# Two wide layers' second product as three sweeps of seven block products, with weight sums added up in DRAM

## The chip, the cores and the metric

The kernel runs on one core of a Trainium2 chip. The time is device microseconds (us) of that core, as the median of several runs. TensorE (PE) does the matmuls, VectorE (DVE), ScalarE (ACT) and GpSimd (POOL) the elementwise work; SyncE (SP), ACT and POOL can issue DMAs.

## What is computed

Two layers of an encoder over 512 tokens of width 1024, in float32. Cut to what matters:

```python
for layer in range(DEPTH):                       # 2
    hn = rmsnorm(h, norm_mix[layer])
    h = h + (hybrid_attention(hn, ...) if layer % 2 == 0 else neighbourhood_attention(hn, ...))
    h = h + sq_relu_mlp(rmsnorm(h, norm_ffn[layer]), ffn_w_up[layer], ffn_w_down[layer])
return rmsnorm(h, final_norm)

def sq_relu_mlp(h, w_up, w_down):                # (512, 1024) x (1024, 4096) x (4096, 1024)
    u = jax.nn.relu(h @ w_up)
    return (u * u) @ w_down
```

"First product" is `h @ w_up`, "second product" is `(u * u) @ w_down`; these are the wide layers.

## The kernel before

Activations lie transposed in SBUF: `hT` holds 8 blocks of 128 features by 512 tokens. Every float32 factor is split into a rounded high part (ACT) and a remainder (DVE or POOL), and a product is three matmuls: high by high, high by low, low by high (lines 500 to 503). 30 slots of 128 x 1024 numbers (`Slot`) hold what lives longer; weights come through `raw`, `whi` and `wlo`. `weights` (line 237) loads five chunks ahead and splits two ahead of the one in use.

The plain form (`product`, line 415) multiplies a 128 x 128 weight block by all 512 tokens. The seven-product form (`Seven`, line 314) takes two 128-row blocks of the sum, two column blocks and two token halves together, as a 2 x 2 block product with seven multiplications in place of eight, each by 256 tokens. For it POOL makes the sums of weight blocks (lines 302 to 304) and of the tokens (336 to 340), and DVE and ACT put the seven results together (396 to 400).

`mlp` (line 1250) goes in stages, by `SIZES`. Layer 0 makes 6 blocks of 128 rows of `u` plainly and multiplies them plainly with `w_down`; then 8 more blocks by the seven-product form, multiplied plainly; then 8 more plainly multiplied and 10 kept, which `convert` turns into five pairs for four runs of the seven-product form, one for every 256 output columns. In layer 1 it is 6, 8 and 6 blocks plainly, 8 in the seven-product form, and 4 at the very end with the tokens as the stationary factor (`down`, line 1621), together with the final norm.

The order within each engine's queue is set by the framework's scheduler, which may move an instruction ahead of others as long as its data allow it; only layer 1's attention (`fixed_order`, line 957) and single instructions (`keep_in_program_order`) stand as written. All DMAs of one engine are issued in the order of its queue, and an instruction that waits holds up all that stand behind it on its engine. Layer 0's attention (`attend`, line 961) works through 64 steps: scores (TensorE), row minimum (DVE), exponential (ACT), reciprocal (DVE), scaling of `p` by it (POOL, line 1005), transposes and values (TensorE). Between the steps `fill` puts matmuls of projections.

Of the kernel before, what the change touches and what calls it, by code (L numbers as in the profile page):

```python
# [35 lines left out]
def encoder_kernel(ctx: ExitStack, tc: tile.TileContext, ins, out, dbg=None):  # L36
# [738 lines left out]

    kst = Slot()
# [312 lines left out]

    fill.add("z", product(w_in, 0, XP, tiles(768, 384), ev_cq, three))  # L1090
# [4 lines left out]
    attend(all_heads(), step)  # L1095
    fill.until("out")
# [11 lines left out]
    SIZES = (6, 8, 8, 10), (6, 8, 6, 8, 4)  # L1108

    def first_product(l):  # L1110
# [10 lines left out]
        state = dict(c=SIZES[l][0], ids=None, plain=False, split=iter(()))  # L1121
# [68 lines left out]
        def stage(n, raw=0, more=0):  # L1190
# [4 lines left out]
            while left:  # L1195
# [5 lines left out]
                for _ in x7.run(i, raw_evac if more <= left < more + raw else pair_evac):  # L1201
                    pass
# [40 lines left out]
    def convert(u7, R):  # L1243
        held = tc.keep_in_program_order
        for kp, raw in enumerate(R):
            yield from u7.sums(kp, raw, DVE, held)
            yield
            yield from u7.split(kp, held)

    def mlp(l, last=None):  # L1250

# [6 lines left out]
        beside = lambda m, i: None  # L1258
        k0 = 0
        for z, n in enumerate(SIZES[l][:3]):  # L1260
            U, R, V = stage(n, *(SIZES[l][3:] if z == 2 else ()))
            up = [s_.pair() for s_ in U]

            def ev(m, b):
                DVE.tensor_tensor(hT[:, m, :], hT[:, m, :], b, op=ALU.add)

            gens = [product(w, k0, up, tiles(512 * c, 512), lambda j, b, c=c: ev(4 * c + j, b)) for c in range(2)]
            k0 += n
            work = iter(())
            if z == 2:  # L1270
                u7 = Seven(2 * len(R))
                ids = [u7.plan(w, 256 * m, k0) for m in range(4)]
                if last:
                    beside = last(k0 + 2 * len(R), V)
                reserve[0] = 8
                work = convert(u7, R)
            else:
                ahead()
            for c, gen in enumerate(gens):
                for i, _ in enumerate(gen):  # L1280
                    if z == 0:
                        later(c, i)
                    elif z == 1:
                        next(bias, None)
                    next(work, None)
            for _ in work:
                pass
            reserve[0] = 1
            for s_ in U:
                s_.free()  # L1290
        for m in range(4):

            def evac(w_):
                h2 = hT[:, 2 * m : 2 * m + 2, :]
                DVE.tensor_tensor(h2, h2, w_.t.rearrange("p (z n) -> p z n", z=2), op=ALU.add)

            for i, _ in enumerate(u7.run(ids[m], evac)):
                beside(m, i)
        u7.free()

    mlp(0)


# [273 lines left out]
    def last_mlp():  # L1577
# [43 lines left out]
        def down(k0, c, up, tail):  # L1621
# [5 lines left out]
            def run():  # L1627
# [27 lines left out]
        def last(k0, tiles_):  # L1655
# [4 lines left out]
            def beside(m, i):  # L1660
                if m == 2 and i == 0:
# [3 lines left out]
                if m > 1 and i in (16, 22):  # L1665
                    turn(2 * (m - 2) + (i == 22), 0)
# [3 lines left out]
        mlp(1, last)  # L1670
# [58 lines left out]
```

## Time and profile before

| | |
|---|---|
| median of 3 runs | 1183.78 us (1182.7 to 1184.34) |
| span of the profiled execution | 1184.0 us |
| TensorE busy, share of the span | 98% |
| VectorE, ScalarE, GpSimd busy | 75%, 54%, 44% |
| granted TensorE clock, mean | 0.994 |
| bytes moved by DMA | 128.01 MB |
| layer 0's attention with its projections | to about 268 us |
| layer 0's wide layer | about 268 to 604 us |
| layer 1's attention | about 604 to 828 us |
| layer 1's wide layer and final norm | about 828 us to the end |

A page of the profile gives busy time by engine, then the DMA queues (q1 is that of SP, q0 of POOL, q10 of ACT), then the chain that ended last and the costliest groups. A group's row reads: line, engine, operation, output and inputs, shape, count, then busy time in all and mean of one in ns, then idle time before it and what ended that. A timeline's row gives the start and the duration first, and in brackets the idle time before it. A windows row gives for a stretch the busy us and the count for each engine, then the granted clock, the share of the DMA engines that was busy, and GB/s.

### The profile page before, as it was taken

To read this page: it belongs to the slowest core of one execution; us is meant where nothing else is said; L and a number is where in the kernel's file an instruction comes from. 1 tells how busy PE (TensorE), PEld (TensorE's weight loads), DVE (VectorE), ACT (ScalarE), POOL (GpSimd) and SP (SyncE) were. 2 spreads that over 40 slices of the span, in tenths; PEclk is the share of its full clock that TensorE was granted. 3 is DMA by queue.
4 is the path that set the end of the run, shared out by engine and by line. 5 is a ranking of instruction groups with operands and counts; after the bars stand their busy time and mean duration, and the time that the engine had idled before them with its cause. 6 is when DMAs were issued, how large, how long until landed. Compare 5 with 4: busy or idle time off the path is not lost.

```text
span 1184.0 us, 19784 instructions
## 1 busy us (share of the span) xinstructions
PE 1160.5 (98%) x7128; PEld 1021.2 (86%) x7128; DVE 883.2 (75%) x1514; ACT 640.3 (54%) x1081; POOL 526.1 (44%) x662
## 2 busy tenths in 40 slices
PE   9989999999999999999999999999999999999997
PEld 8667778888899899988998998988889989998895
DVE  5788998878967368786884676667996736778975
ACT  4468676664546247562553565555554624666344
POOL 3267343224562377819602232231376625774710
PEclk9999999999999999999999999999999999999998
DMA  7223225212524723225226464433352341322412
GB/s 244 71 54 92 68 78 134 62 56 77 167 86 134 263 70 90 72 90 165 67 72 178 131 184 126 116 112 109 107 165 76 115 134 55 98 64 89 143 36 71
DMA packets 110145, 128.01 MB, mean 108 GB/s; under 512 B 9075, under 2 KB 86816, under 8 KB 110048
## 3 DMA queue, kind: packets, MB, share of 16 engines
q1 hardware_dynamic: 106992, 119.30, 33.5%
q0 software_dynamic: 2304, 6.31, 2.2%
q8 instruction: 56, 0.92, 0.3%
q10 hardware_dynamic: 752, 1.15, 0.3%
q14 instruction: 41, 0.34, 0.1%
HBM read 104.32 MB, written 6.29 MB: 93 GB/s over the span
## 4 chain that ended last, share of the span: by engine, by line
PE 81%; DVE 4%; ACT 1%; issue 1%; POOL 0%; DVEq 0%; ACTq 0%
PE mm L503 8%; PE mm L501 8%; PE mm L502 8%; PE mm L390 4%; PE mm L389 4%; PE mm L388 4%; PE t L388 3%; PE t L389 3%; PE t L390 3%; PE s L502 2%; PE s L503 2%; PE s L501 2%; PE s L390 2%; PE s L388 2%; PE s L389 2%; PE s L997 2%
## 5 line engine op out<-in xcount | busy, mean ns | idle before, releaser
L309 DVE TENSOR_TENSOR wlo<-a,whi 128x896 fp32r<-128x896 f32 x132 | 161.8, 1230 | 83.7 <-ACT whi L308 82.9
L308 ACT ACTIVATE whi<-a 128x896 fp32r<-128x896 f32 x132 | 125.0, 950 | 155.0 <-PE o L502 45.8
L501 PE MATMUL mm<-a,whi 128*128 128x512 f32 x485 | 195.9, 406 | 0.9 <-DVE a L915 0.7
L503 PE MATMUL mm<-a,wlo 128*128 128x512 f32 x485 | 192.1, 397 | 2.5 <-DVE wlo L202 2.5
L502 PE MATMUL mm<-a,whi 128*128 128x512 f32 x485 | 192.5, 397 | 0.1
L202 DVE TENSOR_TENSOR wlo<-raw,whi 128x1024 fp32r<-128x1024 f32 (+4 forms) x117 | 139.3, 1193 | 66.4 <-ACT whi L212 63.9
L212 ACT ACTIVATE whi<-raw 128x1024 fp32r<-128x1024 f32 (+3 forms) x120 | 116.4, 971 | 92.2 <-PE s L502 39.8
L302 POOL TENSOR_TENSOR a<-a 128x128 f32<-128x128 f32 x132 | 85.1, 645 | 173.3 <-DMA a<-in_ffn_w_up_dram 103.9
L303 POOL TENSOR_TENSOR a<-a 128x256 f32<-128x256 f32 x132 | 120.2, 910 | 10.3
L304 POOL TENSOR_TENSOR a<-a 128x128 f32<-128x128 f32 x132 | 115.1, 872 | 10.3
L503 PEld LDWEIGHTS mm<-a,wlo 128*128 128x128 f32 x485 | 91.7, 189 | 23.7 <-DVE wlo L202 3.4
L501 PEld LDWEIGHTS mm<-a,whi 128*128 128x128 f32 x485 | 91.8, 189 | 20.4 <-PE t L972 0.9
L502 PEld LDWEIGHTS mm<-a,whi 128*128 128x128 f32 x485 | 91.9, 190 | 17.4 <-DVE a L545 0.4
L388 PE MATMUL mm<-a,whi 128*128 128x256 f32 x370 | 103.9, 281 | 0.0
L389 PE MATMUL mm<-a,whi 128*128 128x256 f32 x370 | 103.9, 281 | 0.0
L390 PE MATMUL mm<-a,wlo 128*128 128x256 f32 x370 | 103.7, 280 | 0.0
L1005 POOL TENSOR_SCALAR p<-p,ti 128x512 f32<-128x512 f32 x64 | 46.2, 724 | 92.3 <-DVE ti L1004 81.1
L1430 POOL TENSOR_SCALAR p<-p,ti 128x256 f32<-128x256 f32 x64 | 35.6, 567 | 104.8 <-DVE ti L1429 91.8
L388 PE MATMUL t<-a,whi 128*128 128x256 f32 x264 | 74.2, 281 | 0.0
L389 PE MATMUL t<-a,whi 128*128 128x256 f32 x264 | 74.1, 281 | 0.0
L390 PE MATMUL t<-a,wlo 128*128 128x256 f32 x264 | 73.9, 280 | 0.0
L390 PEld LDWEIGHTS mm<-a,wlo 128*128 128x128 f32 x370 | 69.6, 188 | 0.2 <-DVE wlo L309 0.2
(338 smaller groups left out, 3210.8 us busy)
## 6 DMA issues: line engine op xcount, KB each, us to landing
a<-in_ffn_w_up_dram SPq DMA_DIRECT2D x104, 256.0 KB
raw<-in_ffn_w_down_dram SPq DMA_DIRECT2D x46, 512.0 KB
raw<-in_od_w_qkv_dram SPq DMA_DIRECT2D x64, 128.0 KB
a<-in_ffn_w_down_dram SPq DMA_DIRECT2D x28, 256.0 KB
raw<-in_ffn_w_up_dram SPq DMA_DIRECT2D x12, 512.0 KB
raw<-in_ev_w_in_dram SPq DMA_DIRECT2D x12, 384.0 KB
a<-a SPq DMA_DIRECT2D x18, 256.0 KB
bias<-bx SPq DMA_DIRECT2D x16, 256.0 KB
```

The costliest lines, as they stand in the source:

```text
L202: z = lambda: (eng or DVE).tensor_tensor(to, src, f32(high), op=ALU.subtract)
L212: ACT.activation(hi[:, 0:m], raw[:, 0:m], AF.Copy)
L303: POOL.tensor_tensor(r[:, 4:6], r[:, 2:3].to_broadcast([P, 2, P]), r[:, 0:7:6], op=ALU.add)
L304: POOL.tensor_tensor(r[:, 7], r[:, 3], r[:, 5], op=ALU.subtract)
L308: ACT.activation(hi[:, 0:896], raw[:, 128:1024], AF.Copy)
L309: DVE.tensor_tensor(lo[:, 0:896], raw[:, 128:1024], f32(hi[:, 0:896]), op=ALU.subtract)
L388: PE.matmul(o, wh, x[:, 0], start=kp == 0 and n in (0, 1, 3, 5), stop=False, skip_group_check=True)
L389: PE.matmul(o, wh, x[:, 1], start=False, stop=False, skip_group_check=True)
L390: PE.matmul(o, wl, x[:, 0], start=False, stop=kp == self.np - 1, skip_group_check=True)
L501: PE.matmul(o, wh, xh, start=first, stop=False)
L502: PE.matmul(o, wh, xl, start=False, stop=False)
L503: PE.matmul(o, wl, xh, start=False, stop=last)
```

## The change

The second product takes six blocks of `u` plainly, as before, and all others (26 in layer 0, 22 in layer 1; in layer 1 four more go to `down` as before) in the seven-product form, in one go: two 128-row blocks by the two halves of the 1024 output columns by two token halves. A pair of blocks needs 7 products with four column blocks each. They are done in three sweeps over all pairs (`kind` 0, 1, 2 with two, two and three products), and each sweep leaves sums in the banks X, Y and Z that later go to `hT`. So the first product makes all its 26 remaining blocks in one row of 13 runs.

The weight sums of the sweeps are made in DRAM, in a copy `made` of the weights: for each pair ACT copies 256 rows (1 MB) from DRAM to DRAM, and POOL issues four DMAs of 256 rows by 256 columns x 2 (0.26 MB) that add to what stands there, two from the weights and two from blocks of `made` itself. There are 13 + 11 pairs. The code asks for one add at each step of layer 0's attention from the fifth step on (layer 0's pairs), and for layer 1's adds beside layer 0's wide layer. POOL no longer makes sums for the second product. The token sums (`one` to `four`) and remainders are on VectorE. The transposes of layer 1's end (`turn(j, 0)`) move from the old last run into `down`.

```diff
+    FIRST, RAW, MORE = 6, (26, 22), (0, 4)
...
+    class SumsAhead:
+            self.made = dr.tile([n, 2, P, 1024], F32, name=nm("made"))
...
+        def steps(self):
+            todo = []
+            for kp in range(self.n + 4):
+                if kp < self.n:
+                    k = self.k0 + 2 * kp
+                    ACT.dma_start(self.made[kp].rearrange("z p c -> (z p) c"), self.w[k * P : (k + 2) * P, :])
+                for back, z, f, src in ((2, 1, 1, lambda q: self.weight(q, 0, 1)), (2, 0, 1, lambda q: self.weight(q, 0, 0)),
+                                        (3, 0, 0, lambda q: self.block(q, 1, 1)), (4, 1, 0, lambda q: self.block(q, 0, 0))):
+                    if 0 <= kp - back < self.n:
+                        POOL.dma_start(self.block(kp - back, z, f), src(kp - back), accum_op=ALU.add)
+                        yield
...
+        if n > 3:
+            next(sums0, None)
+    ahead0, ahead1 = (SumsAhead(ins["ffn_w_down"][l], FIRST, RAW[l] // 2) for l in range(2))
+    sums0, sums1 = ahead0.steps(), ahead1.steps()
...
-    SIZES = (6, 8, 8, 10), (6, 8, 6, 8, 4)
...
+    def sweep_chunk(w, k0, kind, made):
...
+        if kind == 0:
+            for z in range(2):
+                SP.dma_start(line(a[:, S * z : S * z + S]), half(k0 + z, 0))
+        else:
+            for z in range(2):
+                SP.dma_start(line(a[:, S * z : S * z + S]), blocks(made[z])[:, (z, 1 - z)[kind - 1]])
+        if kind == 2:
+            SP.dma_start(line(b[:, 0:S]), half(k0 + 1, 1))
...
+        ACT.activation(hi, a, AF.Copy)
+        DVE.tensor_tensor(lo, a, f32(hi), op=ALU.subtract)
+        third = None
+        if kind == 2:
+            third = Slot()
+            ACT.activation(third.t[:, 0:S], b[:, 0:S], AF.Copy)
+            DVE.tensor_tensor(third.t[:, S:], b[:, 0:S], f32(third.t[:, 0:S]), op=ALU.subtract)
...
+    class Sweeps:
...
+        def tokens(self, kind, kp):
...
+            if kind == 0:
+                split_to(d[:, :, 0], d[:, :, 1], r[:, 0:4:2])
+                self.one(kp)
+                if kp < 2:
...
+            elif kind == 1:
+                for q, src in enumerate((r[:, 0], s2)):
+                    split_to(d[:, q, 0], d[:, q, 1], src)
+                if kp + 2 < self.n:
+                    self.two(kp + 2)
+                if kp + 2 >= self.n:
+                    self.three(kp + 2 - self.n)
+                    self.four(kp + 2 - self.n)
...
+        def run(self, R):
...
+            PRODUCTS = [
+                [(X, 0, at(0)), (Z, 1, at(S))],
+                [(Y, 0, at(S)), (X, 1, at(0))],
+                [(Y, 2, at(S)), (Z, 1, lambda h, m: (h[2].t[:, 0:S], h[2].t[:, S:], P * m)), (X, 0, at(0))],
+            ]
...
+                PE.matmul(o, wh, x[:, 0], start=first and m % 2 == 0, stop=False, skip_group_check=True)
+                PE.matmul(o, wh, x[:, 1], start=False, stop=False, skip_group_check=True)
+                PE.matmul(o, wl, x[:, 0], start=False, stop=last, skip_group_check=True)
...
+            steps = [(kind, kp) for kind in range(3) for kp in range(self.n)]
...
-        for z, n in enumerate(SIZES[l][:3]):
...
+    def mlp_swept(l, made, last=None, sums=iter(())):
...
+        reserve[0] = 3
+        sweeps = []
+        R = stage(0, RAW[l] + MORE[l], 0, lambda: sweeps.append(Sweeps(w, FIRST, made)), lambda: next(sums, None))[1]
...
+        for n, (kind, kp) in enumerate(sweeps[0].run(R)):
+            beside(kind, kp)
+            if n % 16 == 15:
+                next(rest, None)
+            if n % 4 == 0:
+                next(sums, None)
...
+    mlp_swept(0, ahead0, None, sums1)
...
+                if c == 0:
+                    for j in range(4):
+                        turn(j, 0)
...
+            def beside(kind, kp):
+                if (kind, kp) == (2, 6) and not H:
...
+        mlp_swept(1, ahead1, last)
+        flip[0] = 1
```

How the scheduler laid this out is seen in the built programs. First ACT's queue at the program's start, before (`whi` and `a` are high parts, `raw` loaded weights):

```order
L111 DMA cst<-in_cst_dram 128x182
L112 DMA a_82<-in_norm_mix_dram 16x128
L140 ACT_TABLE_LOAD
L140 ACTIVATE ti_109<-zeros 128x1
L1649 ACT_TABLE_LOAD
L1649 ACTIVATE ti_12779<-ones 128x1
L143 ACTIVATE gT<-t_111 128x16
L544 ACTIVATE a_114<-t_155,gT 128x512
L212 ACTIVATE whi_150<-raw_148 128x768
```

and the same place now (`made_621` is layer 0's copy of the weights, `made_622` layer 1's):

```order
L111 DMA cst<-in_cst_dram 128x182
L112 DMA a_82<-in_norm_mix_dram 16x128
L140 ACT_TABLE_LOAD
L140 ACTIVATE ti_109<-zeros 128x1
L802 DMA made_621<-in_ffn_w_down_dram 16x16384 x2
L143 ACTIVATE gT<-t_111 128x16
L212 ACTIVATE whi_150<-raw_148 128x768
L544 ACTIVATE a_114<-t_155,gT 128x512
L544 ACTIVATE a_115<-t_167,gT 128x512
L802 DMA made_621<-in_ffn_w_down_dram 16x16384
L212 ACTIVATE whi_177<-raw_175 128x768
```

The copies (L802) stand between the first loads' splits; 20 of the 24 are issued before ACT takes up `raw_654`, a chunk of the projection that follows the first six column blocks.

POOL's queue behind its first small loads, with the semaphores that each row waits for, before:

```order
L130 DMA a_82<-in_final_norm_dram 8x128
L517 ISA
L517 TENSOR_TENSOR acc_122<-acc_122,sc_248 128x512 [waits Activation_49]
L517 TENSOR_TENSOR acc_122<-acc_122,sc_283 128x512 [waits Activation_49,Pool_49]
L517 TENSOR_TENSOR acc_122<-acc_122,sc_318 128x512 [waits Activation_49,Pool_49]
```

and now (DMAHW are the semaphores of SP's and ACT's DMAs, DMASW those of POOL's, eight of each in turn; a row with `in_ffn_w_down_dram` adds weights, one with `made` on both sides adds a block of the copy):

```order
L130 DMA a_82<-in_final_norm_dram 8x128
L806 DMA made_621<-in_ffn_w_down_dram 256x256 [waits DMAHW5_49,DMASW0_49]
L806 DMA made_621<-in_ffn_w_down_dram 256x256 [waits DMASW1_49]
L806 DMA made_621<-in_ffn_w_down_dram 256x256 [waits DMAHW0_49,DMASW2_49]
L806 DMA made_621<-in_ffn_w_down_dram 256x256 [waits DMASW3_49]
L806 DMA made_621<-made_621 256x256 [waits DMASW4_49,DMASW0_49]
L806 DMA made_621<-made_621 256x256 [waits DMASW5_49,DMASW2_49]
L806 DMA made_621<-in_ffn_w_down_dram 256x256 [waits DMAHW3_49,DMASW6_49]
L517 ISA
L517 TENSOR_TENSOR acc_122<-acc_122,sc_248 128x512 [waits Activation_49]
```

Seven adds stand ahead of POOL's first sum of squares, and each waits for ACT's copy (DMAHW) or for an earlier add (DMASW).

The third place is POOL's queue in layer 0's attention, from the 18th scaling of `p` on, before:

```order
L1005 TENSOR_SCALAR p_1205<-p_1205,ti_1204 128x512
L202 TENSOR_TENSOR wlo_1432<-raw_1054,whi_1431 128x2x256
L705 TENSOR_TENSOR a_1231<-a_1231 128x512
L563 TENSOR_TENSOR sc_1161<-sc_1161,a_132 128x512
L1005 TENSOR_SCALAR p_1246<-p_1246,ti_1245 128x512
L1005 TENSOR_SCALAR p_1277<-p_1277,ti_1276 128x512
L202 TENSOR_TENSOR wlo_1432<-raw_1054,whi_1431 128x2x256
L1005 TENSOR_SCALAR p_1324<-p_1324,ti_1323 128x512
L1005 TENSOR_SCALAR p_1405<-p_1405,ti_1404 128x512
```

and now (line 1038 is the old 1005):

```order
L1038 TENSOR_SCALAR p_1226<-p_1226,ti_1225 128x512
L806 DMA made_622<-in_ffn_w_down_dram 256x256
L202 TENSOR_TENSOR wlo_1460<-raw_1070,whi_1459 128x2x256 x2
L806 DMA made_622<-in_ffn_w_down_dram 256x256
L1038 TENSOR_SCALAR p_1269<-p_1269,ti_1268 128x512
L806 DMA made_622<-made_622 256x256 x2
L563 TENSOR_TENSOR sc_1181<-sc_1181,a_132 128x512
L1038 TENSOR_SCALAR p_1301<-p_1301,ti_1300 128x512
L806 DMA made_622<-made_622 256x256 x2
L1038 TENSOR_SCALAR p_1349<-p_1349,ti_1348 128x512
L806 DMA made_622<-made_622 256x256
L1038 TENSOR_SCALAR p_1431<-p_1431,ti_1430 128x512
```

The last of the 96 adds (layer 1's among them) stands between the 21st and the 22nd of the 64 scalings of `p`; the remaining part of POOL's queue has none.

More of the change, by code (lines that the diff above doesn't have):

```diff
@@ L1291, in mlp, with ev @@
[L1291 to L1301, printed above, removed]
+        U = stage(FIRST)[0]
+        up = [s_.pair() for s_ in U]
+        def ev(m, b):
+            DVE.tensor_tensor(hT[:, m, :], hT[:, m, :], b, op=ALU.add)
+        gens = [product(w, 0, up, tiles(512 * c, 512), lambda j, b, c=c: ev(4 * c + j, b)) for c in range(2)]
@@ L1304, in encoder_kernel @@
+        for _ in bias:
+            pass
+        assert next(rest, 0) == 0 and next(sums, 0) == 0
+        reserve[0] = 1
+    mlp_swept(0, ahead0, None, sums1)
     X = [Slot() for _ in range(KD)]
```

213 lines of the change are left out of this document (167 added, 46 removed).

## The prediction

> **What bounds the kernel now.** I read the page first, then the windows view, then POOL and the DMA queues in the first 120 us, because the build order (shown above) puts the new DMAs there.
>
> ```profile
> span 1184.0 us, 19784 instructions
> ...
> PE 1160.5 (98%) x7128; PEld 1021.2 (86%) x7128; DVE 883.2 (75%) x1514; ACT 640.3 (54%) x1081; POOL 526.1 (44%) x662
> ...
> DMA  7223225212524723225226464433352341322412
> ...
> q1 hardware_dynamic: 106992, 119.30, 33.5%
> q0 software_dynamic: 2304, 6.31, 2.2%
> ```
>
> TensorE is busy 98% of the span, so the kernel lasts as long as its matmuls, wherever nothing makes them wait. The DMA engines are on average a third busy. That average says nothing yet about one stretch of the program, so the windows view gives stretches: the first 120 us, then one with matmuls of 256 columns (340 to 360 and 1000 to 1020) and one with matmuls of 512 columns (380 to 400).
>
> ```profile
> core 0: us, PE busy (x) PEld busy (x) DVE busy (x) ACT busy (x) POOL busy (x), PEclk, DMA share, GB/s
> 0.00:120.00 120.00, 111.04 (x556) 87.02 (x557) 87.58 (x201) 74.51 (x145) 60.39 (x67) 0.99 0.38 114
> 340.00:360.00 20.00, 20.00 (x172) 20.00 (x171) 15.77 (x19) 11.20 (x15) 9.54 (x12) 1.00 0.18 52
> 380.00:400.00 20.00, 20.00 (x88) 16.21 (x87) 10.12 (x13) 7.29 (x8) 5.00 (x9) 1.00 0.73 235
> 1000.00:1020.00 20.00, 20.00 (x172) 20.00 (x171) 16.09 (x21) 13.63 (x18) 11.49 (x16) 1.00 0.32 93
> ```
>
> The counts give the price of a matmul: 20.00/172 = 0.1163 us for 256 columns, 20.00/88 = 0.2273 us for 512. The single durations of matmuls in the group view overlap and would be wrong here. In attention TensorE hardly waits either; this is the wait view from 60 to 250 us, first rows:
>
> ```profile
> PE s L997 <- DVE ti L1001: 2.9, 2, 2.4
> PE s L997 <- DVE a L624: 1.4, 1, 1.4
> PE o L985 <- DVE a L975: 1.2, 3, 0.5
> ```
>
> So a wait put into attention has no slack to disappear in.
>
> **The change, part by part.**
>
> *The matmuls.* In layer 0, 16 blocks of 128 rows leave the plain form (16 x 8 column tiles x 3 = 384 matmuls of 512) and 5 pairs leave the old seven-product form (5 x 4 groups x 7 x 3 = 420 of 256); 13 pairs enter the sweeps (13 x 7 x 4 x 3 = 1092 of 256). In layer 1, 14 blocks (336 of 512) and 4 pairs (336 of 256) leave, and 11 pairs (924 of 256) enter. Together 720 of 512 columns go, worth 720 x 0.2273 = 163.7 us, and 2016 - 756 = 1260 of 256 come, worth 146.5 us. The term is **-17.1 us**. The first product, the plain six blocks and the last four blocks of layer 1 keep their counts. The moved transposes (`turn`) are as many as before.
>
> *What must hide behind the sweeps.* One pair takes TensorE 84 x 0.1163 = 9.8 us. VectorE then has three weight remainders of 1024 columns and one of 512, token remainders (two of 512, three of 256) and four token sums of 256. The group view with shapes kept apart:
>
> ```profile
> L202 DVE TENSOR_TENSOR wlo<-raw,whi 128x1024 fp32r<-128x1024 f32 x88 | 113.2, 1288 | 55.7 <-ACT whi L212 53.4 <-PE o L390 2.2
> L830 DVE TENSOR_TENSOR a<-sc,a 128x512 fp32r<-128x512 f32 x42 | 33.3, 800 | 11.1 <-ACT a L833 11.1
> L363 DVE TENSOR_TENSOR a<-a,a 128x512 fp32r<-128x512 f32 x51 | 41.2, 846 | 0.7 <-ACT a L362 0.7
> L363 DVE TENSOR_TENSOR a<-a,a 128x256 fp32r<-128x256 f32 x17 | 9.7, 573 | 0.0
> ```
>
> With these means it is 3 x 1.288 + 0.800 + 2 x 0.846 + 7 x 0.573 = 10.4 us, above 9.8; that end would cost 24 x 0.6 = 14 us. With the shortest of each kind it is less; the line view's least, median and longest are
>
> ```profile
> L363 DVE TENSOR_TENSOR a<-a,a x68: 406/684/1231, 308.3 to 1105.0; 128x512 fp32r<-128x512 f32 x51, 128x256 fp32r<-128x256 f32 x17
> L830 DVE TENSOR_TENSOR a<-sc,a x42: 673/693/1251, 98.0 to 870.4; 128x512 fp32r<-128x512 f32 x42
> L1295 DVE TENSOR_TENSOR hT<-hT,a x8: 1214/1224/1544, 570.6 to 1154.0; 128x1024 f32<-128x1024 f32 x8
> ```
>
> and 3 x 1.214 + 3 x 0.673 + 7 x 0.406 = 8.5 us. In the sweeps POOL makes no sums any more, so I stand nearer to the short end and cost this at 0, with 14 us as the other end. The weights of a pair are 1.84 MB in 9.8 us, 188 GB/s; the stretch from 380 us moved 235 GB/s at a share of 0.73 without a wait of TensorE, so they hide too.
>
> *Copies and adds.* The sums need 24 copies of 1.05 MB (issued by ACT) and 96 adds of 0.262 MB (issued by POOL): 25.2 MB of copies and another 25.2 MB of adds. The code asks for them step by step, during attention and layer 0's wide layer, but the built order above does not keep this: ACT issues its copies from its fifth row on, and POOL has issued the last add, also of layer 1's sums, after the 21st scaling of `p`. POOL's queue is in order, and an add waits until its copy, and the add it builds on, have landed. So everything that POOL does behind them waits: the remainders, the rotary products, and each scaling of `p`, which TensorE's transposes need. Before, POOL got there at this time (timeline, POOL; the row at 118.99 holds the 21st and 22nd):
>
> ```profile
> 77.62 0.69 POOL L1005 TENSOR_SCALAR p<-p,ti 128x512 f32<-128x512 f32 x1 [6.32 <-DVE ti L1004]
> ...
> 116.13 1.61 POOL L1005 TENSOR_SCALAR p<-p,ti 128x512 f32<-128x512 f32 x2
> 117.71 1.29 POOL L202 TENSOR_TENSOR wlo<-raw,whi 128x512 fp32r<-128x512 f32 x1
> 118.99 2.32 POOL L1005 TENSOR_SCALAR p<-p,ti 128x512 f32<-128x512 f32 x2
> ```
>
> So all of it has to be through by 120 us, or attention is late by the difference. The issue time alone nearly fills POOL: a POOL DMA takes 544 ns in this row,
>
> ```profile
> L1338 POOL DMA_DIRECT2D a<-a x16 | 8.7, 544 | 61.5 <-DVE a L830 56.2 <-ACT p L1460 4.2 <-PE s L1426 1.1
> ```
>
> so 96 of them are 52 us beside the 60.4 us that POOL is busy in the first 120 us. ACT's 24 issues, at the 0.51 us of an issue in SP's queue, are 12 us beside its 74.5 us; they hide in what follows.
>
> ```profile
> 1.24 0.51 SPq L190 DMA_DIRECT2D raw<-in_ev_w_in_dram  x1
> ```
>
> What decides is the data. The first 50 us in 40 slices show what the DMA engines give when they are full (digits of 9):
>
> ```profile
> DMA  0299879999998479993172037006500600000000
> GB/s 0 53 331 344 217 285 391 383 393 392 380 405 322 104 227 416 305 375 125 21 216 86 0 42 272 1 0 125 189 0 14 196 0 0 0 13 0 7 0 8
> ```
>
> Full means about 392 GB/s. The loads of today already take 0.38 x 120 = 45.6 us of all engines by 120 us. The copies take 25.2 MB / 392 GB/s = 64.2 us; the trace has no copy inside DRAM, and this is its nearest row. They could not be free, nor could they add speed. An add is in no row either. Its low end is one pass of its bytes at 392 GB/s, 0.67 us each and 64 us for all. Its high end is the price of a packet in POOL's own queue (q0 above): 2.2% of 16 x 1184 us over 2304 packets is 181 ns, and 96 x 256 rows of 1 KB at 181 ns over 16 engines are 278 us. I take two passes, **128 us**, since an add reads its source and its target before it writes. Rows of 1 KB go slower than 392 GB/s (52 GB/s at a share of 0.18 is 289 GB/s in the window from 340 us), so 128 us is also one and a half passes at that speed.
>
> The sum for the end of the adds: 3 us until transfers begin, 45.6 + 64.2 + 128 = 241 us, less the last eight adds that may still be under way when POOL goes on (eight semaphores, 8 x 1.33 = 11 us): 230 us. Against 120 us that is a delay of **110 us**. Nothing behind gives it back: from 160 us on TensorE was full, and its queue is in order.
>
> The Trainium skill bears on this in two places of the page "DMA: Bandwidth & Descriptors". The section "Issuing engines are not separate DMA queues" says that DMAs issued by SP, ACT and POOL share the same 16 engines. The row of the first 50 us agrees as far as it goes: one queue alone fills all engines. If the rule failed here, the copies and adds would cost nothing, and the sum would be 1167 us. The section "Where 436 GB/s comes from" sets the ceiling at 435 GB/s; by that figure my estimate for 13.7 + 25.2 + 50.4 MB would be 205 us instead of 238.
>
> The whole: 1184.0 - 17.1 + 110 = **1277 us**. The sum is made on the span of the profiled execution, 1184.0 us, which lies 0.2 us from the median of the timed runs, 1183.78 us.
>
> **The rivals.**
>
> *One pass.* An add costs no more than a plain transfer of its bytes. Then 3 + 45.6 + 64.2 + 64.2 - 5 = 172 us, a delay of 52 us, and 1184.0 - 17.1 + 52 = 1219 us. For it: reading and writing may overlap within an engine. Against it: the rows of 1 KB are slower than that even plainly.
>
> *Packet price.* The adds go at POOL's packet price: 3 + 45.6 + 64.2 + 278 - 23 = 368 us, a delay of 248 us, and 1415 us. For it: it is the only row of POOL's queue. Against it: those packets were of 2.7 KB on average and there were few of them.
>
> *The traffic hides (faster).* The engines are 0.38 busy in the first 120 us, so 71 us are free, and if copies and adds fit there, only the matmul term is left: 1184.0 - 17.1 = 1167 us. It decides at the price of an add: the copies leave 120 - 3 - 45.6 - 64.2 = 7 us for no delay at all, and the gain is used up at 7 + 17 = 24 us, which is 0.25 us an add, or 1050 GB/s. No slice reaches half of that. It could still come true if attention had more room than the wait view shows.
>
> *VectorE bounds the sweeps.* This is the 14 us above, on top of any case: 1291 us with the forecast, and 1181 us, within or near no change, if the traffic hides.
>
> That the sums are not spread over the program as the code asks is settled by the order, and part of the forecast.
>
> **How the numbers follow.** Two passes, 1240 to 1330 with its neighbours: 0.50. One pass, 1205 to 1240: 0.22. Packet price, 1330 to 1420: 0.14; beyond that 0.06. The traffic hides, 1167 us: 0.06, and with VectorE's 14 us: 0.02. The range from 1205 to 1420 leaves out the last three, 0.14. About 0.2% is what a measurement of this kernel can tell from no change. Faster by more than that is the 0.06; within it 0.02; slower 0.92.
>
> **What would show it.** Right: in the changed profile the DMA row stands at 9 from the start to about 230 us; POOL's L806 rows carry waits of some hundred us in sum; the 22nd scaling of `p` starts near 230 instead of 121 us; TensorE's idle time before 250 us grows by about 110 us; and from the end of attention on, the program is about 17 us shorter than before. The matmul step is wrong if the sweeps do not run at 172 matmuls per 20 us. The forecast is wrong if the last L806 has been issued by 135 us: then the traffic did hide. An add's time from issue to landing tells one pass from two and from the packet price.

## The result, and the profile after

The changed kernel took 1305.1 us (median of 4 runs, 1304.3 to 1305.7) against 1184.1 us for the kernel before on the same chip: a ratio of 1.102, 95% interval 1.100 to 1.104. The forecast was 1277 us, with a range of 1205 to 1420.

First the page of the profile after: the span, the engines' busy time, two of its rows of 40 slices (32.6 us each), and the DMA queues with packets, MB and share of 16 engines.

```profile
span 1303.7 us, 21309 instructions
...
PE 1172.4 (90%) x7668; PEld 1053.0 (81%) x7668; DVE 911.8 (70%) x1627; ACT 676.9 (52%) x1157; POOL 526.7 (40%) x650
...
PE   6706276799999999999989999999999999999997
...
DMA  9999999931412342237578254654343423266712
...
q1 hardware_dynamic: 134736, 138.18, 35.3%
q0 software_dynamic: 28416, 31.48, 15.1%
q10 hardware_dynamic: 1520, 26.32, 5.1%
```

TensorE fell from 98% to 90% of the span, and all of it is lost in the first eight slices, where the DMA row stands at 9. Two queues tell the price of the new transfers. q10 (ACT's) carried 0.3% without the copies (the run without sums, below), so the copies cost 5.1% x 1303.7 - 0.3% x 1166.7 = 63 us of the 16 engines. q0 (GpSimd's) carried 2.2% of 1184.0 us before, so the adds cost 15.1% x 1303.7 - 26 = 171 us, 1.78 us each.

The windows view of the same run shows where the time came in. It is cut at the first scaling of `p` (185 us), behind the last one (387 us), and at 461.7 us, inside layer 0's wide layer, where ScalarE first splits a weight of the seven-product form.

```profile
core 0: us, PE busy (x) PEld busy (x) DVE busy (x) ACT busy (x) POOL busy (x), PEclk, DMA share, GB/s
0.00:185.00 185.00, 92.08 (x328) 67.40 (x328) 56.19 (x117) 37.80 (x65) 79.92 (x92) 0.71 1.07 264
185.00:387.00 202.00, 178.15 (x982) 146.10 (x982) 149.81 (x345) 127.28 (x268) 107.12 (x124) 0.92 0.60 127
387.00:461.70 74.70, 74.49 (x329) 60.28 (x328) 65.01 (x87) 39.01 (x61) 36.46 (x36) 1.00 0.33 100
461.70:1303.70 842.00, 827.73 (x6033) 779.21 (x6031) 640.82 (x1079) 472.84 (x766) 303.21 (x401) 1.00 0.46 137
```

In the first 185 us TensorE ran 328 matmuls, where the run without sums ran 928, and the DMA share is 1.07 (the packet times of several queues are added up, so it can pass 1 where they overlap). From 461.7 us on nothing is lost to the sums: the run without sums takes 842.70 us for the same part (6035 matmuls). That the sweeps themselves keep their pace is seen further down.

The line view of L806 in the profile after has its durations, its first and last issue, the idle time ahead of it, and the time to landing.

```profile
L806 POOL DMA_DIRECT2D made<-in_ffn_w_down_dram x48: 872/1541/3798, 9.9 to 247.4; - x48
L806 POOL DMA_DIRECT2D made<-made x48: 869/896/4142, 18.5 to 259.0; - x48
...
  DMA made<-in_ffn_w_down_dram: 65.2, 10
  DMA made<-made: 32.3, 14
...
DMA to landing us min/median/max: 4.8/9.7/37.7
```

The last add is issued at 259.0 us, and GpSimd stood 97.5 us at adds, waiting for landings. Its timeline from 55 us on shows how attention's work stands between them.

```profile
55.78 1.79 POOL L806 DMA_DIRECT2D made<-made  x2 [8.27 <-DMA made<-in_ffn_w_down_dram]
56.94 1.93 POOL L517 TENSOR_TENSOR acc<-acc,sc 128x512 f32<-128x512 f32 x1
58.16 2.45 POOL L806 DMA_DIRECT2D made<-in_ffn_w_down_dram  x2
71.62 0.88 POOL L806 DMA_DIRECT2D made<-made  x1 [11.01 <-DMA made<-in_ffn_w_down_dram]
85.84 0.88 POOL L806 DMA_DIRECT2D made<-made  x1 [13.34 <-DMA made<-made]
```

A sum of squares (L517) gets through at 56.94, and then nothing but adds for 30 us. Landings of copies and adds (the outputs named `made`) take 10% of the span on the chain that ended last. The scalings of `p` of the changed kernel, all 64 and those from 259 us on:

```profile
L1038 POOL TENSOR_SCALAR p<-p,ti x64: 687/696/3814, 185.5 to 381.0; 128x512 f32<-128x512 f32 x64
...
L1038 POOL TENSOR_SCALAR p<-p,ti x43: 687/693/1922, 259.6 to 381.0; 128x512 f32<-128x512 f32 x43
```

Before, the first came at 77.6 and the last at 244.3 us. The last is 136.7 us late. Once the adds are out of the way the 43 that are left take 121.4 us; without sums, 44 take 125.4 us (118.3 to 243.7). So the whole delay has come about by the time the last add is issued.

### The profile page after: what moved, and what is told of

It is laid out like the page before. It is cut to its first block, busy times and chain, and to the rows that moved or that the text cites. A ratio compares the mean times of both kernels' runs of the same rounds, so it can differ in the third digit from the quotient of the medians.

```text
span 1303.7 us, 21309 instructions
## 1 busy us (share of the span) xinstructions
PE 1172.4 (90%) x7668; PEld 1053.0 (81%) x7668; DVE 911.8 (70%) x1627; ACT 676.9 (52%) x1157; POOL 526.7 (40%) x650
## 3 DMA queue, kind: packets, MB, share of 16 engines
q0 software_dynamic: 28416, 31.48, 15.1%
## 4 chain that ended last, share of the span: by engine, by line
PE 76%; DMA 13%; DVE 4%; issue 2%; POOL 2%; ACT 2%; SPq 0%; DVEq 0%; POOLq 0%; ACTq 0%
DMA made<-in_ffn_w_down_dram 6%; PE mm L503 6%; PE mm L501 6%; PE mm L502 6%; DMA made<-made 4%; PE t L1407 3%; PE t L1409 3%; PE t L1408 3%; PE mm L389 3%; PE mm L388 3%; PE mm L390 3%; PE s L1030 2%; PE o L1018 2%; PE t L389 2%; PE t L388 2%
## 5 line engine op out<-in xcount | busy, mean ns | idle before, releaser
L502 PE MATMUL mm<-a,whi 128*128 128x512 f32 x395 | 162.5, 412 | 26.4 <-DVE a L545 26.4
L501 PE MATMUL mm<-a,whi 128*128 128x512 f32 x395 | 165.4, 421 | 21.6 <-ACT a L544 21.3
L309 DVE TENSOR_TENSOR wlo<-a,whi 128x896 fp32r<-128x896 f32 x98 | 125.1, 1279 | 52.4 <-ACT whi L308 51.8
L202 DVE TENSOR_TENSOR wlo<-raw,whi 128x1024 fp32r<-128x1024 f32 (+4 forms) x87 | 104.3, 1204 | 67.1 <-ACT whi L212 66.8
L308 ACT ACTIVATE whi<-a 128x896 fp32r<-128x896 f32 x98 | 92.9, 950 | 105.9 <-PE o L502 22.9
L212 ACT ACTIVATE whi<-raw 128x1024 fp32r<-128x1024 f32 (+3 forms) x90 | 84.6, 942 | 106.9 <-DMA raw<-in_ev_w_in_dram 28.7
L502 PEld LDWEIGHTS mm<-a,whi 128*128 128x128 f32 x395 | 78.2, 198 | 42.9 <-DVE a L545 28.2
L501 PEld LDWEIGHTS mm<-a,whi 128*128 128x128 f32 x395 | 77.7, 198 | 39.3 <-ACT a L544 22.7
L806 POOL DMA_DIRECT2D made<-made x48 | 62.4, 1406 | 99.6 <-DMA made<-in_ffn_w_down_dram 59.8
L1038 POOL TENSOR_SCALAR p<-p,ti 128x512 f32<-128x512 f32 x64 | 65.4, 1139 | 75.8 <-DVE ti L1037 62.4
L503 PEld LDWEIGHTS mm<-a,wlo 128*128 128x128 f32 x395 | 78.2, 198 | 18.1 <-issue 0.6
L304 POOL TENSOR_TENSOR a<-a 128x128 f32<-128x128 f32 x98 | 84.5, 862 | 7.7
L302 POOL TENSOR_TENSOR a<-a 128x128 f32<-128x128 f32 x98 | 62.6, 639 | 54.5 <-DMA a<-in_ffn_w_up_dram 19.2
L1305 DVE TENSOR_TENSOR wlo<-a,whi 128x1024 fp32r<-128x1024 f32 x53 | 65.4, 1237 | 20.9 <-ACT whi L1304 20.6
L389 PE MATMUL mm<-a,whi 128*128 128x256 f32 x280 | 78.5, 280 | 0.0
L388 PE MATMUL mm<-a,whi 128*128 128x256 f32 x280 | 78.4, 280 | 0.0
```

Source lines behind the costliest of these rows:

```text
L202: z = lambda: (eng or DVE).tensor_tensor(to, src, f32(high), op=ALU.subtract)
L308: ACT.activation(hi[:, 0:896], raw[:, 128:1024], AF.Copy)
L309: DVE.tensor_tensor(lo[:, 0:896], raw[:, 128:1024], f32(hi[:, 0:896]), op=ALU.subtract)
L388: PE.matmul(o, wh, x[:, 0], start=kp == 0 and n in (0, 1, 3, 5), stop=False, skip_group_check=True)
L389: PE.matmul(o, wh, x[:, 1], start=False, stop=False, skip_group_check=True)
L501: PE.matmul(o, wh, xh, start=first, stop=False)
```

## The experiments

The question was by which way 171 us of adds and 63 us of copies became 138 us: by GpSimd's queue, by the DMA engines themselves, or by the landings that adds wait for; and whether another place for them hides them.

**Without sums.** The sweeps read plain weights of the same shape.

```
-            self.made = dr.tile([n, 2, P, 1024], F32, name=nm("made"))
+            self.made = [w[(k0 + 2 * q) * P : (k0 + 2 * q + 2) * P, :].rearrange(...) for q in range(n)]
-                    ACT.dma_start(self.made[kp]..., self.w[k * P : (k + 2) * P, :])
-                        POOL.dma_start(self.block(kp - back, z, f), src(kp - back), accum_op=ALU.add)
```

> The 24 copies and the 96 adds are left out; the sweeps read plain weights of the same shape, so the output lacks the weight sums. Capacity theory (the copies and adds use up the 16 DMA engines at the program's start and hold the attention back through GpSimd's queue): the last scaling of p falls back from 380.25 to about 243.6 us, and the time is 1305.1 - 136.7 = 1168 us, 16 us under the kernel before, the matmul term alone. Rival (the sweeps' own loads and VectorE work carry a good part of the loss): the attention comes back, but the time stays over 1184 us.

1167.2 us, a ratio of 0.985 (0.982 to 0.989). The line view of this run, all 64 scalings of `p`:

```profile
L1038 POOL TENSOR_SCALAR p<-p,ti x64: 691/696/1652, 77.6 to 243.7; 128x512 f32<-128x512 f32 x64
```

And its windows view for the part that starts at 461.7 us in the changed kernel:

```profile
324.00:1166.70 842.70, 830.51 (x6035) 781.93 (x6033) 641.90 (x1079) 472.76 (x766) 307.97 (x404) 0.99 0.46 137
```

The scalings are back where they were, and what is left is a gain of 16.7 us on the 1183.95 us of the kernel before: the matmul term with whatever the sweeps lose. So the sums cost 1305.1 - 1167.2 = 137.9 us.

**Copies only.** The adds are left out (the last line above alone).

> The 96 adds are left out, the 24 copies stay; the output lacks the weight sums. Capacity theory: loads and copies together are 3 + 45.6 + 66.5 = 115 us of the 16 engines, just under the 120 us that the stage took before, so the delay is small: 1168 to 1185 us. Rival (the copies, first in the queues, push the loads of the first projections back by their own length): 1168 + 66 = 1234 us.

1195.4 us, ratio 1.010 (1.008 to 1.012): 28.2 us for copies that should have fitted, below the rival's 66 and above the range of the capacity theory. The chain of waits of this run has these two pieces near its start (start, length, what):

```profile
18.43 18.04 DMA raw<-in_ev_w_in_dram
36.53 20.55 DMA raw<-in_ev_w_in_dram
```

The first weights, which lead the program, come late behind copies of 1 MB. That happens with no add in GpSimd's queue. The page "DMA: Bandwidth & Descriptors" of the Trainium skill says, under "Issuing engines are not separate DMA queues", that DMAs of all issuers interleave on the same 16 engines; this run agrees: with ACT's copies beside them two of SyncE's loads stand on the chain with 18.0 and 20.6 us, and ScalarE waits 7.3 us for such loads in the first 100 us, 1.1 us without copies and adds.

**Plain transfers in place of adds.**

```
-                        POOL.dma_start(self.block(kp - back, z, f), src(kp - back), accum_op=ALU.add)
+                        POOL.dma_start(self.block(kp - back, z, f), src(kp - back))
```

> The 96 adds become plain copies of the same 256 KB in the same order with the same waits; the output lacks the weight sums. Capacity theory with an add that goes through the engines about twice: one transfer falls from 1.78 us to 0.9 us of the 16 engines (1 KB rows at 289 GB/s), 96 of them from 171 to 87 us, the last is issued at about 259 - 84 = 175 us, and the time is 1305 - 84 = 1221 us, up to 1242 us if the loads take some of the time set free. Latency theory (the queue's waits for landings set the pace, not the engines): the waits are the same, 1290 to 1305 us. The share of the software queue falls from 15.1% to about 9% in the first case.

1265.2 us, ratio 1.068 (1.065 to 1.071). The price came out as expected and the time did not. The row of GpSimd's queue on this run's page:

```profile
q0 software_dynamic: 9984, 31.48, 8.7%
```

The line view of L806 of the same run, issues and idle time ahead of them:

```profile
L806 POOL DMA_DIRECT2D made<-in_ffn_w_down_dram x48: 557/559/613, 10.7 to 210.0; - x48
L806 POOL DMA_DIRECT2D made<-made x48: 557/559/669, 17.4 to 218.9; - x48
...
  DMA made<-in_ffn_w_down_dram: 60.4, 13
  DMA made<-made: 15.6, 7
```

8.7% x 1263.3 - 26 = 84 us, 0.87 us each: an add costs twice a plain transfer of the same rows. That saved 87 us of the engines and only 39.9 us of time, so the remaining 69.8 us over the copies alone are lost to plain transfers too. From 120 to 220 us the engines' share here is 0.76, and GpSimd still waits 76 us for landings.

**No chain, with adds and with plain transfers.** All four of a pair read from the weights.

```
-   (3, 0, 0, lambda q: self.block(q, 1, 1)), (4, 1, 0, lambda q: self.block(q, 0, 0))):
+   (3, 0, 0, lambda q: self.weight(q, 0, 1)), (4, 1, 0, lambda q: self.weight(q, 0, 0))):
```

> All four adds of a pair read from the weights, none from a sum, so that no add waits for another add's landing at its source; bytes, rows and count are the same, the output has wrong sums. Capacity theory: the engines are as full as before, 1295 to 1305 us. Latency theory: the 32 us that GpSimd waited at the adds for earlier adds' landings go, 1270 us or less.

> The adds as plain copies, and all four of a pair from the weights, so that none waits for another's landing at its source; the output lacks the weight sums. With the chain, plain copies gave 1265 us, their last issued at 218.9 us, the engines at 0.66 to 0.90 from 120 us on. If the landings of the chain left the engines idle there: capacity alone gives 3 + 45.6 + 66.5 + 84 = 199 us for the last, a delay of 79 us behind the 120 us, 1167 + 79 = 1246 us. If what holds the queue back is each pair's wait for its own copy: as with the chain, 1260 to 1265 us.

1293.8 us with adds (ratio 1.092, 1.086 to 1.098) and 1257.1 us with plain transfers (1.061, 1.059 to 1.064). The chain of landings is worth 11 and 8 us; it is not the cause. GpSimd still stood 76.7 us (35 times) and 60.4 us (31 times) at L806 for transfers from the weights, that is, for copies or for earlier transfers of its own (the profile gives both the same name).

**Attention's work off GpSimd.** (GpSimd is POOL in the views.) L517, L562, L563, L595, L705, L1038 and the split of one projection (L1128) go to VectorE, then also the splits asked for in L873 to L875.

```
-            POOL.tensor_scalar(p, p, t[:, 3:4], 1.0, op0=ALU.mult, op1=ALU.mult)
+            DVE.tensor_scalar(p, p, t[:, 3:4], 1.0, op0=ALU.mult, op1=ALU.mult)
```

> Copies and adds stand as in the changed kernel, in front; the work that attention gives GpSimd (square sums, rotations, the scalings of p, some of the splits) is done on VectorE instead, so that no work of attention stands behind an add in a queue. Nothing is left out. If GpSimd's queue is the way by which the adds reach the path: what stays is the loads' share, as with the copies alone (25 us) and somewhat more for the adds' traffic, the first scaling of p at 110 to 130 us, 1200 to 1230 us in all, VectorE's added 80 us included. If the way is the DMA engines, whose full queues hold back loads and moves: the first scaling of p at 160 us or later, 1260 us or more.

1322.8 us, ratio 1.117 (1.115 to 1.120), slower than the changed kernel. The wait view of TensorE in this run (sum, times, longest) shows one wait that is longer than all others:

```profile
PE s L1030 <- DMA a<-sc: 82.0, 2, 76.5
```

The wait view of SyncE says what held that move:

```profile
SPq L190 <- POOL wlo L202: 87.9, 3, 85.3
```

Three kinds of splits (L202) had stayed on GpSimd, behind the adds. SyncE's load into the buffer that such a split frees waited 85.3 us, and the next head's move of its query halves (`a<-sc`) stood behind that load in SyncE's queue. So this run does not tell the theories apart; it shows how one stopped queue stops another. The second run removes the splits:

> As with attention's work taken off GpSimd, where three kinds of splits (L873 to L875) had stayed on it behind the adds and one move stood 76.5 us behind them through SyncE's queue; these are on VectorE now too, so that no work of attention stands behind an add. Nothing is left out. If GpSimd's queue is the main way to the path: the wait of 76.5 us goes, and the time is 1200 to 1250 us. If the full DMA engines alone, by stretching attention's loads and moves, cost what the changed kernel lost: 1290 us or more. Between the two both ways count, about as the time divides the stretch from 1195 us (copies alone) to 1305 us.

1261.6 us, ratio 1.065 (1.062 to 1.069). The line view of L806 of this run:

```profile
L806 POOL DMA_DIRECT2D made<-made x48: 872/878/1928, 19.2 to 256.2; - x48
```

The chain of waits of this run has four loads of the first weights in it, of which these are the third and the fourth:

```profile
43.55 23.85 DMA raw<-in_ev_w_in_dram
83.43 31.43 DMA raw<-in_ev_w_in_dram
```

The scalings of `p` of this run, now VectorE's, from 260 us on:

```profile
L1038 DVE TENSOR_SCALAR p<-p,ti x29: 469/479/487, 260.7 to 341.1; 128x512 f32<-128x512 f32 x29
```

With no work of attention in GpSimd's queue the last add is still issued at 256.2 us, and GpSimd still waits 153 us for landings at L806, so the adds set their own pace. Attention runs beside them, but slowly: 35 of its 64 scalings are done by 260 us, where the run without sums had finished. The 29 that are left take 80.4 us, and the last 32 of the run without sums took 84.4 us (159.3 to 243.7), 2.87 and 2.72 us from one to the next, so VectorE's added work costs little there. What is lost is lost beside the adds: 1261.6 - 1195.4 = 66.2 us over the copies alone, by way of loads and moves on the same engines. On the chain up to 280 us the loads of weights make 94.3 us here and 52.6 us with the copies alone, the moves 36.0 and 15.8 us; ScalarE waits 35.4 us for the first weights in the first 100 us, 7.3 us with the copies alone. GpSimd's queue adds 1305.1 - 1261.6 = 43.5 us.

**Other places.** First half of the work left in front, then all of it held where the code asks.

```
-                        POOL.dma_start(self.block(kp - back, z, f), src(kp - back), accum_op=ALU.add)
+                        tc.keep_in_program_order(POOL.dma_start(..., accum_op=ALU.add))
```

(and the copies alike; in the first of the two for layer 1 only).

> Only layer 1's copies and adds are held at the places at which the code writes them; layer 0's go ahead as in the changed kernel. Nothing is left out. Capacity theory: loads 45.6, half of the copies 33, half of the adds 86 us, 168 us with the 3 us of start for the last add of layer 0, a delay of 48 us, 1167 + 48 = 1215 us. If the delay came from the number of adds ahead of the scalings rather than from the engines' time, or from the latency of the first landings: 1235 us or more.

> Copies and adds are held at the places at which the code writes them: layer 0's over its attention, layer 1's over layer 0's MLP. Nothing is left out. Capacity theory with GpSimd's queue as the way to the path: no add stands ahead of the scalings of p in bulk, the engines have about 0.7 of their time free there (they stood at 0.1 to 0.5 between 60 and 260 us without the sums), the 171 us of adds find room, and the time is that without sums, 1167 to 1180 us, under the kernel before. Rival (adds cost the path wherever they stand, through contention with the weight loads or through GpSimd's time of 0.9 to 1.5 us each): 1200 us or more.

Layer 1 held: 1251.4 us, ratio 1.056 (1.054 to 1.059); layer 0's share in front delays the last scaling by 68.7 us (to 312.4) against the run without sums, and layer 1's, held over layer 0's MLP, costs another 15 us there. The 1215 us of the capacity theory fell. All held: 1228.5 us, ratio 1.038 (1.035 to 1.041), the last scaling at 286.3, 42.6 us late, and again 14 us in the MLP. The expectation of 1167 to 1180 us fell. The timeline of the held order at the first burst of copies:

```profile
80.04 1.16 ACTq L802 DMA_DIRECT2D made<-in_ffn_w_down_dram  x2
...
82.63 0.50 SPq L636 DMA_DIRECT2D a<-sc  x1
...
93.97 0.46 SPq L637 DMA_DIRECT2D a<-sc  x1
...
100.21 0.77 PE L1030 MATMUL s<-a,a 128*128 128x512 f32 x1 [16.69 <-DMA a<-sc]
```

A move of 128 KB within the chip's buffers, on the path to the next head's scores, came late beside copies of 1 MB (and, from 85.77 us on, the first adds), and TensorE waited 16.7 us for it. Such waits come to 22.7 us in attention; how the rest of the 42.6 us came about is not shown. In the MLP the trace points to GpSimd's own time (windows view):

```profile
460.00:500.00 40.00, 35.76 (x286) 34.20 (x286) 23.95 (x27) 21.76 (x26) 37.89 (x49) 1.00 0.63 137
```

It is busy 37.9 of 40 us with the sums of the first product and the adds among them, and TensorE makes 286 matmuls instead of 344. No run takes the sums of the first product off GpSimd, so this cause is argued and not shown.

**The bias stores.** Held order, with 48 stores moved from SyncE's queue (`SP.dma_start` to `POOL.dma_start` at L1270, L1274 and L1276), which I took for the cause of a dip of 6 us in layer 0's sweeps.

> The held order, and the 48 stores of layer 1's bias are issued from GpSimd's queue, not from SyncE's, where they stand in 30 us of layer 0's sweeps ahead of the sweeps' weight loads. If those stores are what loses 6 us of TensorE there (145 matmuls in each of two 20 us windows, 172 elsewhere): 6 us under the held order alone, 1161 to 1174 us. If the loads are late for another reason: no difference.

1229.3 us, ratio 1.038 (1.036 to 1.040): no difference. In the run's windows the dip stays,

```profile
590.00:610.00 20.00, 13.01 (x89) 12.51 (x88) 9.73 (x13) 9.76 (x15) 2.66 (x5) 0.74 0.57 173
```

so SyncE's queue was not its cause. It stands right after, or in, a window in which the engines' share is near 1 (0.97 here, 1.00 in the run without sums); whether the stores' traffic makes it was not tried.

**Small steps.** Copies in parts of 256 KB, one part and one add at a time, layer 0's at attention's 64 steps, layer 1's over layer 1's attention.

```
+                for part, (back, z, f, src) in enumerate(order):
+                    if kp < self.n:
+                        k, r = self.k0 + 2 * kp, 64 * part
+                        held(ACT.dma_start(self.made[kp].rearrange("z p c -> (z p) c")[r : r + 64], ...))
+                    if 0 <= kp - back < self.n:
+                        held(POOL.dma_start(self.block(kp - back, z, f), src(kp - back), accum_op=ALU.add))
+                    yield
```

> Nothing is left out. Each copy goes in four parts of 256 KB, one part and one add at a time, held in program order: layer 0's over its 64 attention steps, layer 1's over layer 1's own attention (64 places), where GpSimd is busy 2 to 3 tenths and the engines have half their time free, not over layer 0's first product, where GpSimd is busy 19 of 20 us. If what the held order lost (42.6 us up to the last scaling of p, 14 us in layer 0's MLP) were the bursts of 1 MB copies ahead of small moves (one wait of 16.7 us for a<-sc) and GpSimd's time in the first product: the last scaling of p at 243.7 to 260 us, and 1167 to 1184 us in all. If each add delays the path's small moves wherever it stands: the last scaling at 270 us or later, and 1195 us or more.

1255.6 us, ratio 1.060 (1.057 to 1.062), worse than the held order. GpSimd waits only 2.9 us for landings at its adds now, and yet the last scaling comes at 310.3 us, 66.6 us late. Layer 1's attention, with layer 1's sums beside it, takes 186.1 us from its first to its last scaling of `p`, 166.0 us without sums, and so loses another 20 us. The chain of waits of this run, its DMA pieces from 85 to 280 us (start, length, what):

```profile
86.96 2.81 DMA a<-a
89.83 4.47 DMA a<-sc
141.62 6.46 DMA sc<-in_ev_w_in_dram
155.34 5.43 DMA a<-a
160.78 4.12 DMA a<-sc
188.24 5.63 DMA a<-a
193.88 5.67 DMA a<-a
262.04 3.23 DMA a<-a
265.92 8.07 DMA a<-a
274.01 2.24 DMA a<-a
```

These sum to 48.1 us, 40.9 us of them from 141 us on. The chain of the run without sums reaches back only to 139.7 us; from there to 280 us none of its printed pieces is a DMA, and in its first 260 us TensorE waits for no DMA at all. Attention has a chain of small moves from head to head, and with copies and adds on the engines these moves stand on the path. How much each was stretched, and where the other 18.5 us of the 66.6 went, is not shown.

**Layer 1 alone.** Layer 0's second product as before, layer 1's sums in small steps over layer 0's MLP (`mlp(0, None, sums1)` in place of `mlp_swept(0, ahead0, None, sums1)`, with the old `mlp`).

> Only layer 1's second product in sweeps; layer 0's as in the kernel before. Layer 1's 44 copy parts and 44 adds, one of each at a time, held over layer 0's MLP, where no move of attention is on the path, the engines are 0.2 to 0.7 busy and TensorE does not wait. Nothing is left out. The matmul term of layer 1 alone is 14 of the 30 chunks that change, 14/30 of 16.7 = 7.8 us. If only attention's moves and GpSimd's queue in it make the sums dear: 1176 to 1180 us, a few us under the kernel before. If adds cost the MLP too, through GpSimd's 0.9 us each beside its own sums (14 us when held there in the held order): 1184 us or more.

1221.9 us, ratio 1.033 (1.030 to 1.036), 38 us above the 1184 us at which the second expectation begins. Behind layer 1's last scaling of `p` the run is 12.4 us shorter than the kernel before (363.5 and 375.9 us), more than the 7.8 us expected; layer 0's MLP, between the two attentions, is 47.4 us longer. The windows view of this run in the stretch that lost most:

```profile
380.00:480.00 100.00, 64.81 (x311) 52.72 (x311) 23.97 (x27) 18.57 (x21) 48.36 (x67) 0.83 0.91 233
```

The kernel before in the same stretch:

```profile
380.00:480.00 100.00, 100.00 (x677) 92.04 (x676) 61.86 (x71) 47.57 (x58) 62.23 (x84) 1.00 0.46 144
```

The engines were 0.46 busy here, and TensorE did not wait. With half the sums beside it, the share is 0.91 and TensorE loses 35 us; `DMA bx<-a` (the bias stores) is 35.1% of the chain from 370 to 480 us, and GpSimd is busy less than before (48.4 and 62.2 us), so that GpSimd's busy time does not explain this loss.

## Why the prediction was right or wrong

The side and the mechanism's start were right: the new DMAs go out at the program's start, fill the engines, and attention starts when they are through. The forecast was 28 us low.

| step | forecast | measured |
|---|---|---|
| matmul term | -17.1 us | -16.7 us (without sums) |
| sweeps hide VectorE and the loads | 0 us (other end 14) | 172 matmuls in 20 us, but for one dip of about 6 us |
| copies, time of the engines | 64.2 us | 63 us |
| adds, time of the engines | 128 us, 1.33 each | 171 us, 1.78 each |
| issue of an add on GpSimd | 544 ns | 896 and 1541 ns (medians of the two kinds) |
| last add issued | 230 us | 259.0 us |
| delay | 110 us | 137.9 us (last scaling of `p` 136.7 us late) |

**The matmul term came near partly by luck.** The line views of layer 1's scaling of `p`, before and in the run without sums, split it by layer:

```profile
L1430 POOL TENSOR_SCALAR p<-p,ti x64: 471/482/1697, 641.8 to 808.1; 128x256 f32<-128x256 f32 x64
L1650 POOL TENSOR_SCALAR p<-p,ti x64: 471/482/1697, 637.7 to 803.7; 128x256 f32<-128x256 f32 x64
```

By the prediction's counts layer 0 should give 9.1 us and layer 1 8.0 us. From layer 0's last scaling to layer 1's first it was 397.5 us before and 394.0 us without sums, a gain of 3.5 us; from layer 1's last scaling to the end 375.9 and 363.0 us, a gain of 12.9 us. The dip takes about what layer 0 lacks. Why layer 1 gave 4.9 us more than its matmuls are worth is open.

The sweeps' pace is seen in the changed kernel's first sweep of layer 0 (windows view):

```profile
597.00:617.00 20.00, 20.00 (x172) 20.00 (x171) 20.00 (x35) 15.34 (x20) 0.00 (x0) 1.00 0.95 305
```

TensorE makes its 172 matmuls, but VectorE is busy all 20 us of this window. The work hid with hardly any room, as the two ends of the prediction's sum for VectorE had it, 8.5 and 10.4 us against 9.8 us of TensorE.

**The step that was mis-sized is the price of an add.** "I take two passes, 128 us" had the passes right, since an add cost twice a plain transfer in the same rows (1.78 and 0.87 us), and their speed wrong: 0.26 MB in 0.87 us is 300 GB/s, close to the 289 GB/s of the rows of 1 KB that stood in the prediction, not 392. With 2 x 48 = 96 adds at 1.78 us the sum gives 3 + 45.6 + 63 + 171 - 14 = 269 us, and the last add was issued at 259. So the add was 43 us too cheap and the rest of the sum about 10 us too dear, which brought the forecast nearer. The issue of a DMA on GpSimd was taken from a plain one; plain transfers in the same place took 559 ns, so that row was good for them, but not for adds.

**A step that was incomplete: only GpSimd's queue as the way.** "Everything that POOL does behind them waits" is shown, and it accounts for 43.5 us of the 137.9. The copies alone cost 28.2 us without an add in that queue, and the adds cost another 66.2 us when nothing of attention stood behind them. The two shares depend on the order in which they are taken away; that both count is shown. The sum with one way came near because it timed the last add, and in the changed kernel both the stopped queue and the full engines end with it (259.0 us, and the DMA row's eight slices of 9 to 261 us).

**The rivals.** One pass is refuted by the price; the packet price too (16 x 171 us over 26112 packets is 105 ns, not 181). VectorE did not bound the sweeps, if only just. The traffic that hides was given 0.08, with 0.25 us an add as the point at which it decides. That point was wrong, since it took the copies to fit without a delay: with no adds at all the kernel took 1195.4 us, slower than before, because copies that fit by the sum still made the first loads late. No other place hid them: in front 1305.1, held as written 1228.5, in small steps 1255.6, layer 1 alone 1221.9 us. None of these beats the kernel before.

Of what was to be seen, these came true: the DMA row full to the last add, 97.5 us of GpSimd's waits at L806, the 22nd scaling right after it (259.6 us), 100 us more idle time of TensorE before 250 us, 922.7 us behind attention's last scaling in place of 939.7, and 172 matmuls in 20 us of the sweeps outside the one dip.

**What stays open.** How the 66.2 us divide between late loads and slow moves: the chains put 42 us more on loads and 20 us more on moves, but no run separates them. Why small steps cost more than the held order's bursts (the chain shows moves of 2 to 8 us one after another in the one, the timeline one long wait in the other, but no run changes only that). And the dip of about 6 us in layer 0's sweeps, which every version with sweeps in layer 0 has.

## What to carry to other kernels

A stretch whose DMA engines are a third busy is not two thirds free, if its path runs through loads and moves one after another: here 63 us of copies cost 28 us and 171 us of adds 110 us. Price an added transfer first by its place: what stands behind it in its issuer's queue, and what small transfer on the path will share the engines with it. An add made by a DMA cost two plain transfers of its own rows here, so take the row of the trace with the same row length.

## What the runs showed that was not expected

- The price of an accumulating DMA inside DRAM was nearly the same in three places: 1.78 us for 256 KB in rows of 1 KB in front, 1.87 us in the held order (16.8% of 1223.2 us, less 26, over 96), 1.76 us for layer 1 alone. A plain one took 0.87 us.
- Its issue held GpSimd 0.86 us at the least; a plain one's 557 ns. In the changed kernel the issue of an add took up to 4.1 us; with attention's work off GpSimd and the engines as full, up to 2.4 us. Why is not shown.
- TensorE's granted clock was 0.71 in the first 185 us of the changed kernel, where TensorE was busy half the time, and 0.99 in the same 185 us without sums. Its 328 matmuls there took 281 ns each on the mean; without sums the first 270 took 209 ns each (56.4 us, at a clock of 1.00). Whether this lengthened the run is not shown, since TensorE waits there anyway.
